# One 1 MB load for four column groups, instead of two 512 KB loads for two each, in the modulation rows of a two-block network

## The chip, the cores and the metric

The kernel runs on one core of a Trainium2 chip. The metric is device time in microseconds: the time from the first to the last instruction of one launch, as the median of several runs.

## The reference

The network has two blocks. The first one is two layers of attention and a mixture of experts over 512 tokens of width 1024. The second one is two layers of mixers and feed-forward, and every layer of it is modulated by rows that depend on two small vectors, c and c_ctx. The change is in the computation of these rows alone:

```python
xc = ctx
for layer in range(DEPTH):
    mod = jax.nn.silu(c) @ w_ada[layer] + b_ada[layer]
    sh1, sc1, g1, sh2, sc2, g2 = jnp.split(mod[:, None, :], 6, axis=-1)
    modc = jax.nn.silu(c_ctx) @ w_ada[layer] + b_ada[layer]
    sh1c, sc1c, g1c, sh2c, sc2c, g2c = jnp.split(modc, 6, axis=-1)
    u = modulate(rmsnorm(x, norm_mix_g[layer]), sh1, sc1) @ w_in[layer]
    ...
```

Each layer has 6144 columns of float32 weights over 1024 rows, 25 MB, so 50 MB are read for four rows of results. Around it, and at the same time, runs the first layer of the first block: a sliding window attention of 512 tokens, with 16 query heads and 4 key heads, and a projection of its output.

## The kernel before

The program is traced by Python functions, and a list scheduler then sets the order of instructions on every engine (the context is opened with `schedule_with_timeline_sim=True`). Engines run their own queue in order. SyncE (SP) issues the loads and stores, also in order, so an issue that waits for a buffer holds up all issues behind it.

`whole` calls `swa` (the attention of the first layer), and then `ada` on a second stream of work, `beside`, which lies on the other side of SBUF and has two banks of PSUM, a and b. The scheduler mixes both: between the products of the attention stand those of `ada`. The attention has three parts: the projections of q, k and v (products called mm<-wh,xTh and so on, L232 to L234), the heads themselves (sc<-kT,qT L377, softmax, transposes tp<-cst,pm L424, and po<-pT,v L429), and `out_proj` (mm<-wh,oTh), which ends in a layer norm and the router. Its weights w_o come as eight loads of 512 KB through three buffers. Then the experts follow: `stream` and `weights_of` load their weights; 24 granules called we lie in bytes on the second stream's side and can be loaded before the experts begin. The routing ends in a gather of token rows on GpSimd (L746), which the experts' first product (L795) needs.

`ada` keeps silu(c) and silu(c_ctx) as columns of a tile sT, padded to 32 columns. For each of the two layers and of three parts of 2048 columns it takes eight steps k over the rows. In a step, two loads of 1024 columns (512 KB, four buffers named g) are followed by two products each. A product has sT as its weights, 32 columns wide, and 512 columns of g as the moving operand; its result lies on 32 partitions of the bank (q = 0, 32, 64 or 96), so that the four 512-column pieces of a part fill the bank's 128 partitions. Each float32 product is two instructions of TensorE in the trace. The products are traced at high priority. After the eighth step the bank is added to the biases (row, L1001), and the rows go to DRAM (mod<-row), from where `columns` reads them back (mrow<-mod).

Of the kernel before, what the change touches and what calls it, by code (L numbers as in the profile page):

```python
# [11 lines left out]
F32 = mybir.dt.float32  # L12
# [11 lines left out]
def shape_constants():  # L24
    """Packed [128, n] float32 constants that depend on shapes alone: name -> array."""
# [67 lines left out]
CONST_AT = {}  # name -> group, first column, columns  # L93
# [11 lines left out]
def bcast_rows(ap, n, parts=128):  # L105
    """[n] of DRAM read by every partition."""
    return bass.AP(tensor=ap.tensor, offset=ap.offset, ap=[[0, parts], [1, n]])


def finished(steps):  # L110
    """what a generator returns at its end"""
    while True:
        try:
            next(steps)
        except StopIteration as end:
            return end.value


def together(main, rest):
    """the steps of main, and between them as many of rest as main asks for"""  # L120
# [9 lines left out]
class Net:  # L130
# [10 lines left out]
    def beside(self):  # L141
        """a second stream of work on the other side of SBUF, with two banks of PSUM"""
# [5 lines left out]
    def after(self, engine="PE"):  # L148
        """work traced under what the result returns does not come before what an engine has so far"""
# [8 lines left out]
    def new_x(self):  # L158
        """the four token tiles, in 16 KB that the attentions' outputs use in between"""
        x = self.hp.tile([128, 4, 1024], F32, name="x", tag="x")  # L160
        return [x[:, t] for t in range(4)]
# [16 lines left out]
    def dma(self, out, src):  # L178
        """a load; those of the stream beside go first, as few as they are"""
# [4 lines left out]
    def granule(self, shape):  # L184
        """4 KB of a partition for streamed weights"""
        return self.wp.tile(shape, F32, name="w", tag="w")

    def load_w(self, src, size=1024):
        """src: DRAM AP [128, kc, n] -> per k the two parts [128, n]"""
# [18 lines left out]
    def psum(self, es, **banks):  # L208
        """PSUM for a phase: 2 banks per kind of use, or as told"""
# [5 lines left out]
    def stage(self, whp=0, side=None):  # L215
        """SBUF pools of one stage, on bytes that other stages use at other times"""
# [8 lines left out]
    def split(self, hi, lo, src):  # L225
        """src (float32, SBUF or PSUM) -> hi + lo, both float32r"""
# [9 lines left out]
    def transpose_in(self, tiles, T):  # L236
        """token tiles [128, 1024] -> x^T parts [128, 8, T]"""
# [12 lines left out]
    def dense_tok(self, aT, w, tiles, kc, n, tag="mm"):  # L250
        """aT: parts [128, kc, T]; w: parts; yields (tile index, psum [128, n])"""
# [8 lines left out]
    def rstd(self, var, eps, n=1, scale=1.0):  # L260
        """(scale var + eps) ** -0.5, [128, n]: a first guess from the exponent, then a cubic iteration and Newton's (u: 2/3 of the root)"""
# [28 lines left out]
    def layer_norm(self, x, sums, gb, ta, tb, eps=1e-5):  # L290
        """x [128, 1024] in place; sums: the sum of each row in one or two parts; ta, tb: scratch"""
# [11 lines left out]
    def rope_half(self, out, src, cos, sin, nh, rot, off):  # L303
        """rotate [.., off:off+rot] of src [128, nh, d] into out; cos, sin [128, rot]"""
# [11 lines left out]
    def swa(self, xt):  # L316
        """xt in place; the logits of the experts' router"""
# [10 lines left out]
    def _swa(self, xt, oT):  # L328
# [36 lines left out]
        def attend(s, qT, t):  # L365
            """heads 8s .. 8s+7 of token tile t"""
# [26 lines left out]
    def sink_softmax(self, pm, mx, nh, nk, scale, sink=None):  # L393
        """pm [128, nh, >=nk] masked raw scores, mx raw maxima -> probabilities in place"""
# [21 lines left out]
    def pv(self, pm, nh, nk, v_of, out):  # L416
        """o^T of nh heads (pairs of 64 rows) = sum over key tiles -> out"""
# [15 lines left out]
    def out_proj(self, oT, w_o, i, xs):  # L433
        """the token tiles xs <- layer_norm(alpha x + o @ w); the logits of the experts' router"""
# [24 lines left out]
    def router(self, x, wr, lg):  # L459
        """logits of a token tile"""  # L460
# [12 lines left out]
    def token_parts(self, aT):  # L473
        """a^T [128, 8, T] -> per token tile its two parts [128, 8, 128]"""
# [6 lines left out]
    def reload(self, t):  # L481
        """a token tile from DRAM"""
# [5 lines left out]
    def mla(self, xt):  # L488
        """the new token tiles -> xd; the logits of the experts' router"""
# [1376 lines left out]
```

## Time and profile before

| | |
|---|---|
| time, median of 3 runs | 3500.92 us (3488.79 to 3513.75) |
| span of the profiled execution | 3507.8 us |
| PE busy in the span | 3240.1 us, 92% |
| DVE, ACT, POOL busy | 1666.1, 1164.3, 242.5 us |
| DMA moved | 716.17 MB, mean 204 GB/s |
| mean granted clock of TensorE | 0.963 of full speed |

No time outside the span was recorded for the profiled execution; its span is 0.2% over the median. The change lies in the first 300 us: `ada` begins its products at 23.4 us and ends them at 245 us, the output projection ends at 299 us, and the first expert's product starts at 336 us. Up to there PE is busy almost without a break. In the rows, "idle before" stands in square brackets behind a row with the engine or transfer that ended it.

### The profile page before, as it was taken

Reading aid. Unit: us, or ns where it says so; the run is one execution under the profiler, and the core shown is the slowest. Engines: PE = TensorE matmul, PEld = TensorE weight load, DVE = VectorE, ACT = ScalarE, POOL = GpSimd, SP = SyncE. Lnnn points to the kernel's source line nnn. Section 1 sums busy time; section 2 is a strip of 40 time slices with the busy share of each in tenths; the row PEclk is TensorE's granted clock in tenths of the full one; section 3 lists DMA queues with packets and bytes.
Section 4 is the critical chain, followed back from the end, with each engine's and each line's share of the span. In section 5 each row is a group of like instructions: output and inputs, shape, how many; then the busy total and the mean of one; then the engine's idle time right before and its main releaser. Section 6 shows DMA issues by size and latency. Waiting matters only on the chain. (4 is left out here: it accounts for less than half of the span.)

```text
span 3507.8 us, 48762 instructions
## 1 busy us (share of the span) xinstructions
PE 3240.1 (92%) x18404; PEld 2183.5 (62%) x18404; DVE 1666.1 (47%) x4004; ACT 1164.3 (33%) x2216; POOL 242.5 (7%) x318
## 2 busy tenths in 40 slices
PE   9987999999979979999989859999999899989998
PEld 5445344544476645666625447767888787678887
DVE  2354224223266544544524156556555556655555
ACT  3231212223155414323223144345242443443322
POOL 0000101000000010010010000130000000400000
PEclk9998999999999979999999979989999999899999
DMA  7778998999851489998899932223233232233331
GB/s 255 253 234 342 372 371 310 340 337 340 322 181 32 158 301 304 315 333 273 278 347 351 357 107 79 74 72 108 85 96 92 82 89 71 66 100 94 95 95 55
DMA packets 428088, 716.17 MB, mean 204 GB/s; under 512 B 42984, under 2 KB 283672, under 8 KB 427848
## 3 DMA queue, kind: packets, MB, share of 16 engines
q1 hardware_dynamic: 412872, 691.98, 57.3%
q0 software_dynamic: 14976, 21.02, 2.6%
q8 instruction: 147, 2.41, 0.3%
q14 instruction: 93, 0.76, 0.1%
HBM read 691.76 MB, written 37.87 MB: 208 GB/s over the span
## 5 line engine op out<-in xcount | busy, mean ns | idle before, releaser
L228 DVE TENSOR_TENSOR wl<-w,wh 128x1024 fp32r<-128x1024 f32 (+3 forms) x360 | 425.3, 1188 | 298.1 <-ACT wh L227 275.5
L227 ACT CAST wh<-w 128x1024 fp32r<-128x1024 f32 (+3 forms) x360 | 362.6, 1016 | 585.1 <-PE po L234 148.9
L795 PE MATMUL sc<-wx,xg 128*64 128x512 f32 x1492 | 437.3, 603 | 7.6 <-DMA wx<-in_moe_w_up 7.0
L232 PE MATMUL mm<-xTh,wh 128*128 128x512 f32 (+1 forms) x672 | 262.3, 390 | 1.6 <-ACT xTh L227 1.1
L234 PE MATMUL mm<-xTh,wl 128*128 128x512 f32 (+1 forms) x672 | 261.4, 389 | 1.0 <-DVE wl L228 1.0
L233 PE MATMUL mm<-xTl,wh 128*128 128x512 f32 (+1 forms) x672 | 260.6, 388 | 0.0
L795 PEld LDWEIGHTS sc<-wx,xg 128*64 128x64 f32 x1492 | 121.5, 137 | 193.9 <-issue 158.5
L232 PE MATMUL po<-wh,gTh 128*128 128x256 f32 (+1 forms) x608 | 183.4, 302 | 6.1 <-ACT gTh L227 3.9
L233 PE MATMUL po<-wl,gTh 128*128 128x256 f32 (+1 forms) x608 | 182.1, 300 | 0.0
L234 PE MATMUL po<-wh,gTl 128*128 128x256 f32 (+1 forms) x608 | 182.0, 301 | 0.0
L732 POOL DMA_INDIRECT acc<-y,to x64 | 103.7, 1620 | 1048.4 <-ACT y L809 1013.3
L807 PE MATMUL mm<-wx,hT 128*64 128x512 f32 x580 | 156.8, 657 | 11.5 <-DVE hT L803 7.9
L798 DVE TENSOR_TENSOR hid<-hid,sc 64x512 f32<-64x512 f32 x64 | 44.3, 692 | 236.3 <-ACT hid L797 235.7
L232 PEld LDWEIGHTS mm<-xTh,wh 128*128 128x128 f32 x672 | 127.7, 190 | 32.6 <-issue 2.3
L234 PE MATMUL sc<-xTh,wl 128*128 128x512 f32 (+1 forms) x384 | 145.6, 379 | 0.0
L232 PE MATMUL sc<-xTh,wh 128*128 128x512 f32 (+1 forms) x384 | 145.5, 379 | 0.0
L234 PEld LDWEIGHTS mm<-xTh,wl 128*128 128x128 f32 x672 | 127.7, 190 | 28.5 <-DVE wl L228 1.5
L233 PE MATMUL sc<-xTl,wh 128*128 128x512 f32 (+1 forms) x384 | 145.1, 378 | 0.0
L233 PEld LDWEIGHTS mm<-xTl,wh 128*128 128x128 f32 x672 | 127.6, 190 | 27.1 <-issue 0.7
L232 PE MATMUL a<-xTh,wh 128*128 128x256 f32 (+2 forms) x472 | 139.3, 295 | 2.1 <-ACT wh L227 0.9
L234 PE MATMUL a<-xTh,wl 128*128 128x256 f32 (+2 forms) x472 | 135.5, 287 | 0.8 <-DVE wl L228 0.8
L797 ACT ACTIVATE hid<-sc 64x512 f32<-64x512 f32 x64 | 37.7, 590 | 294.5 <-PE sc L795 294.3
(510 smaller groups left out, 6770.2 us busy)
## 6 DMA issues: line engine op xcount, KB each, us to landing
wx<-in_moe_w_up SPq DMA_DIRECT2D x192, 512.0 KB
wx<-in_moe_w_gate SPq DMA_DIRECT2D x181, 512.0 KB
wx<-in_moe_w_down SPq DMA_DIRECT2D x145, 512.0 KB
w<-in_ffn_w_up SPq DMA_DIRECT2D x264, 256.0 KB
g<-in_w_ada SPq DMA_DIRECT2D x96, 512.0 KB
w<-in_moe_w_down SPq DMA_DIRECT2D x76, 512.0 KB
w<-in_w_in SPq DMA_DIRECT2D x70, 512.0 KB
w<-in_ffn_w_down SPq DMA_DIRECT2D x64, 512.0 KB
```

The costliest lines, as they stand in the source:

```text
L227: self.nc.scalar.copy(hi, src)
L228: self.nc.vector.tensor_tensor(lo, src, hi.bitcast(F32), op=ALU.subtract)
L232: mm(ps, ah, bh, start=start, stop=False)
L233: mm(ps, ah, bl, start=False, stop=False)
L234: mm(ps, al, bh, start=False, stop=stop)
L732: nc.gpsimd.indirect_dma_start(out=acc, out_offset=bass.IndirectOffsetOnAxis(ap=ix, axis=0), in_=y, in_offset=None, bounds_check=1023, oob ...
L795: nc.tensor.matmul(ps[r], xg[:, k], w, start=k == 0, stop=k == 7)
L797: nc.scalar.activation(hid[64:], ps[:64], AF.Silu)
L798: V.tensor_tensor(hid[64:], hid[64:], ps[64:], op=ALU.mult)
L807: nc.tensor.matmul(py[64 * h:64 * h + 64], hT[:, k], w[:, 512 * h:512 * h + 512], start=k == 0, stop=k == 3)
```

## The change

A step now has one load of 2048 columns (1 MB, as a tile of 4 by 512 columns) and four products, one for each 32-partition group, traced one after another. There are two buffers of 8 KB a partition each in place of four of 4 KB, so the bytes are the same. Comments and docstrings were taken out as well, which moves line numbers by three below it (the products' line is L993 after, L995 before; the load's L990 and L991).

```diff
-            wp = self.pool(es, "adw", 4)
+            wp = self.pool(es, "adw", 2)
...
                 for b in range(3):
                     ps = self.bank("mm")
                     for k in range(8):
-                        for h in range(2):
-                            c = 2048 * b + 1024 * h
-                            g = wp.tile([128, 1024], F32, name="g")
-                            nc.sync.dma_start(g, w[:, k, c:c + 1024])
-                            with self.tc.high_priority():
-                                for a in range(2):
-                                    q = 64 * h + 32 * a
-                                    nc.tensor.matmul(ps[q:q + 32], sT[:, k], g[:, 512 * a:512 * a + 512], start=k == 0,
-                                                     stop=k == 7)
+                        g = wp.tile([128, 4, 512], F32, name="g")
+                        nc.sync.dma_start(g, w[:, k, 2048 * b:2048 * b + 2048].rearrange("p (a n) -> p a n", a=4))
+                        with self.tc.high_priority():
+                            for a in range(4):
+                                nc.tensor.matmul(ps[32 * a:32 * a + 32], sT[:, k], g[:, a], start=k == 0, stop=k == 7)
```

The scheduler writes another order. On PE, the products of `ada` (a<-g,sT) stand in 87 places before and in 47 after; 18 of the 48 steps now stand among the projections and up to the first scores, 27 in the heads' part and 3 in the output projection, where before all of them stood ahead of the output projection. From the experts on, the products of PE are the same, with some of the second stream's moved by some places among those of the first layer's experts.

In the heads' part of the attention, PE stood in this order before:

```order
L995 MATMUL a<-g,sT 32x512 x2
L377 MATMUL sc<-kT,qT 128x256
L424 MATMUL tp<-cst_58,pm 128x128 x4
L995 MATMUL a<-g,sT 32x512 x4
L429 MATMUL po<-pT,v 64x128 x4
L377 MATMUL sc<-kT,qT 128x256 x2
L995 MATMUL a<-g,sT 32x512 x2
```

The same engine after, at the same place:

```order
L993 MATMUL a<-g,sT 32x512 x4
L377 MATMUL sc<-kT,qT 128x256 x2
L429 MATMUL po<-pT,v 64x128 x8
L993 MATMUL a<-g,sT 32x512 x4
L377 MATMUL sc<-kT,qT 128x256 x2
L424 MATMUL tp<-cst_58,pm 128x128 x8
L993 MATMUL a<-g,sT 32x512 x4
```

Blocks of four products now stand about twice as far apart as the blocks of two did.

SP's queue at the end of `ada`, before (w_o are the output projection's weights, prow, mrow and cols belong to `columns`, we are the experts' weights):

```order
L181 DMA prow<-in_gla_norm_g 1x64 x2
L439 DMA wr<-in_moe_w_group 128x8x4
L440 DMA wr<-in_moe_w_expert 128x8x32
L181 DMA w<-in_a_w_o 128x2x512 x3
L181 DMA cols<-col 128x320
L832 DMA we<-in_moe_w_gate 128x1024
```

And after, first at the last loads of `ada` and then some 20 rows further on:

```order
L990 DMA g<-in_w_ada 128x2048
L181 DMA w<-in_a_w_o 128x2x512
L990 DMA g<-in_w_ada 128x2048
L181 DMA w<-in_a_w_o 128x2x512 x4
L181 DMA mrow<-mod 16x128 x2
```

```order
L181 DMA mrow<-mod 16x128
L181 DMA mod<-row 2x512 x2
L287 DMA w<-in_ln_g 128x1024
L287 DMA w<-in_ln_b 128x1024
L832 DMA we<-in_moe_w_gate 128x1024
L832 DMA we<-in_moe_w_up 128x1024
```

The last five loads of w_o moved ahead of the small transfers of `columns`, and the first experts' weights moved behind the two loads of the layer norm, which before stood among them.

At the ends of the eight-step sums, SP's queue before:

```order
L991 DMA g<-in_w_ada 128x1024 x16
L181 DMA mod<-row 2x512 x4
L991 DMA g<-in_w_ada 128x1024 x3
L181 DMA row<-in_b_ada 32x512 x4
L991 DMA g<-in_w_ada 128x1024 x13
```

And after:

```order
L990 DMA g<-in_w_ada 128x2048 x8
L181 DMA mod<-row 2x512 x4
L990 DMA g<-in_w_ada 128x2048
L181 DMA row<-in_b_ada 32x512 x4
L990 DMA g<-in_w_ada 128x2048 x7
```

One load of two buffers now stands between the stores of a finished part and the bias loads of the next one, where three of four buffers did.

## Rows read from the trace of the kernel before

**Rows 1.** Busy time in four stretches: length, engines with (instructions), clock, DMA share, GB/s.
```profile
23.30:118.90 95.60, 95.60 (x409) 51.66 (x408) 21.19 (x55) 20.43 (x33) 0.00 (x0) 1.00 0.73 245
118.90:245.30 126.40, 119.80 (x739) 48.68 (x740) 67.57 (x315) 47.63 (x176) 0.00 (x0) 1.00 0.81 259
245.30:299.10 53.80, 49.23 (x218) 38.78 (x218) 26.64 (x61) 12.77 (x16) 0.00 (x0) 0.97 0.86 321
299.10:336.30 37.20, 14.65 (x146) 12.98 (x144) 22.58 (x87) 5.78 (x10) 2.28 (x2) 0.68 0.79 300
```

**Rows 2.** The same view for the instructions of tile g alone (PE, PEld).
```profile
23.30:118.90 95.60, 32.42 (x128) 4.57 (x128) 1.00 0.73 245
118.90:245.30 126.40, 61.14 (x256) 8.56 (x256) 1.00 0.81 259
```

**Rows 3.** PE in order of time: start, us, engine, line, operation, count.
```profile
44.26 0.39 PE L233 MATMUL mm<-wl,xTh 128*128 128x512 f32 x1
44.58 1.05 PE L995 MATMUL a<-g,sT 128*32 128x512 f32 x4
45.56 0.50 PE L234 MATMUL mm<-wh,xTl 128*128 128x512 f32 x1
45.90 0.39 PE L232 MATMUL mm<-wh,xTh 128*128 128x512 f32 x1
46.13 0.39 PE L233 MATMUL mm<-wl,xTh 128*128 128x512 f32 x1
...
118.91 1.06 PE L995 MATMUL a<-g,sT 128*32 128x512 f32 x8
```

**Rows 4.** Who PE waited for, 118.9 to 245.3: us in total, times, longest.
```profile
PE a L995 <- DMA g<-in_w_ada: 6.0, 5, 2.3
```

**Rows 5.** The same for PE's weight loads, its two longest waits for softmax.
```profile
PEld sc L377 <- DVE pm L414: 5.5, 9, 0.8
PEld sc L377 <- DVE mx L379: 5.1, 8, 0.8
```

**Rows 6.** SP and PE in order of time, around a load that PE waited for.
```profile
197.26 1.06 PE L995 MATMUL a<-g,sT 128*32 128x512 f32 x8
198.36 4.11 SPq L991 DMA_DIRECT2D g<-in_w_ada  x4
199.48 1.05 PE L995 MATMUL a<-g,sT 128*32 128x512 f32 x4
...
201.05 1.05 PE L995 MATMUL a<-g,sT 128*32 128x512 f32 x4
...
204.92 1.05 PE L995 MATMUL a<-g,sT 128*32 128x512 f32 x4 [1.60 <-DMA g<-in_w_ada]
```

**Rows 7.** SP around the output projection, in order of time.
```profile
253.91 1.54 SPq L181 DMA_DIRECT2D w<-in_a_w_o  x3
...
258.95 0.42 SPq L832 DMA_DIRECT2D we<-in_moe_w_gate  x1
...
277.06 0.33 SPq L287 DMA_DIRECT2D w<-in_ln_b  x1
```

**Rows 8.** ACT there: the split of w_o's fourth granule.
```profile
258.56 1.04 ACT L227 CAST wh<-w 128x1024 fp32r<-128x1024 f32 x1 [9.04 <-DMA w<-in_a_w_o]
```

**Rows 9.** PE there.
```profile
259.66 0.74 PE L232 MATMUL mm<-wh,oTh 128*128 128x512 f32 x2 [2.10 <-ACT wh L227]
260.92 0.65 PE L233 MATMUL mm<-wl,oTh 128*128 128x512 f32 x1 [0.52 <-DVE wl L228]
```

**Rows 10.** Busy time in two stretches there, columns as in rows 1.
```profile
262.00:264.00 2.00, 2.00 (x6) 1.51 (x6) 1.11 (x3) 0.00 (x0) 0.00 (x0) 0.50 0.98 336
260.00:300.00 40.00, 39.48 (x171) 31.57 (x169) 20.64 (x49) 8.51 (x11) 0.00 (x0) 0.96 1.02 397
```

**Rows 11.** GpSimd's first gather, and the first expert's product, in order of time.
```profile
322.93 1.26 POOL L746 DMA_INDIRECT x<-xd,slots  x1 [322.50 <-DMA wx<-in_moe_w_up]
...
336.29 1.09 PE L795 MATMUL sc<-we,xg 128*64 128x512 f32 x2
```

## Prediction

> **What bounds the kernel now.** I read the busy time by stretches first, since shares of the whole span say nothing of a stage that ends after 300 us. From the first product of `ada` to the first scores PE is busy for 95.60 of 95.60 us, and in the heads' part for 119.80 of 126.40 us, both at full clock [rows 1]. In the heads' part DVE works 67.57 us and ACT 47.63 us, so neither is near its limit, and the DMA engines move 245 and 259 GB/s, where with deep queues they move 397 [rows 1, 10]. PE idles for 6.6 us of the heads' part, and 6.0 of these are waits of `ada`'s products for their weights [rows 4]. So PE bounds these 222 us, and whatever leaves its queue shortens them, until loads or the softmax come late. What `ada` holds of PE is 32.42 + 61.14 = 93.56 us [rows 2]: more than a third of the two stretches, for 48 steps.
>
> **Four groups at once.** A block of two products takes 1.05 us (four instructions). Where two such blocks happen to be neighbours, eight instructions take 1.06 us [rows 3]: all four column groups run beside each other, and the second pair costs 0.01 us. The change makes every step such a block. 48 x 1.06 = 50.9 us in place of 93.56: **-42.7 us**, all of it on the engine that sets the end.
>
> The Trainium skill (TensorE: Matmul & The Clock Gate, Part 3: Packing small matmuls) gives the span of a pack as one matmul plus some 4 ns for each further tile, but lists only 2.38 times for three column groups, 79% of three. By that share a block of four would take about 1.06 / 0.79 = 1.34 us, an estimate, and 13 us of the gain would go. The trace agrees with the span and not with the share: 1.06 against 1.05 us.
>
> **Fewer changes between the two kinds of products.** From 44.26 to 45.90 one ordinary product, one block and one ordinary product begin in turn: 1.64 us; two ordinary steps of 0.23 us (45.90 to 46.13) off, the block costs 1.18, that is 0.13 more than its own 1.05 [rows 3]. 87 places become 47: 40 x 0.13 = **-5.2 us**. Together -47.9.
>
> **Loads.** Bytes in flight stay at 2 MB, but two buffers hold them. A buffer's loop is load, block, next load. No row shows a 1 MB load. The lower bound is from a load that finds the DMA engines idle: the first of three 512 KB loads of w_o is issued at 253.91 and its split begins at 258.56, 4.65 us [rows 7, 8]. The other 512 KB at 397 GB/s add 1.3: 5.95, with the block 7.0, so two buffers give a step every 3.5 us. The upper bound is a load that PE waited for: the block at 197.26 held two buffers and freed them for the loads from 198.36 on; after two more blocks, at 204.92, PE waits for the first of these: 6.56 us [rows 6]. With 1.3 and 1.06 that is 8.9, a step every 4.46 us.
>
> Against this stands PE's own work per step. Projections: (95.60 - 32.42) / 18 steps = 3.51, with the block's 1.19 it is 4.70 us, above both bounds, so no wait there beyond unlucky spacing. Heads: (119.80 - 61.14) / 27 = 2.17, with 1.19 it is 3.36 us, below both [rows 1, 2]. The waits of the heads' part are thus between 27 x 0.14 = 4 us and 27 x 1.10 = 30 us. I take 13, nearer to the lower bound, because at most one other load can stand ahead of a load now, where three could. In this lies also that at the five ends of eight-step sums only one load stands in SP's queue between the stores of mod and the bias loads, which wait for these stores. 6.0 us of waits are there today: **+7 us** net, from -6 (all hidden) to +24.
>
> The Trainium skill (DMA: Bandwidth & Descriptors, Rules for kernel authors) asks for 1 MiB or more a DMA for full bandwidth. By it the larger loads would be faster in themselves, and the waits would go as in the first rival below, 3451 us. The trace shows 397 GB/s with loads of mostly 512 KB [rows 10], so I give the size no credit.
>
> **Softmax.** With PE's part of the heads at 27 x 3.36 = 91 us, plus waits some 104, DVE's 67.57 us become 65% of it, in chains from scores to transposes. Today these waits end under running products: the two longest groups of weight loads that wait for DVE hold 10.6 us, with next to no idle PE [rows 5]. Blocks of `ada` that took two places between scores and transposes take one now, so some cover is gone: **+4 us**, from 0 to 11.
>
> **Output projection.** Today w_o's fourth granule is issued late, behind the small transfers of `columns`; PE waits 2.10 and 0.52 us for its split [rows 9], and then runs at half clock (0.50, the 1.2 GHz level, from 262 to 264), after these idle times, which costs at least 1.0 us more [rows 10]. After the change it is issued ahead of them. But the last two blocks of `ada` stand within this projection, and the very last load is issued only behind that granule, which waits for the split of the first one: **-2 us**, from -3.6 to +4.
>
> **The experts' weights.** In SP's queue their first loads now stand behind ln_b, today at 277.06, instead of at 258.95 [rows 7]: 18 us later in the projection. What covers it: the DMA engines idle for 21% of the 37.2 us from 299.1 to 336.3, 7.8 us [rows 1], and the first product on these weights comes at 336.29 [rows 11]. What isn't covered goes behind the routing's gather (322.93 to the product, 13.4 us, in part queueing behind such loads): **+4 us**, from 0 to 18 - 7.8 = 10.
>
> **Later.** Some products of the second stream change places among the first layer's experts, where PE and DMA are both nearly full: 0, from -10 to +10. Everything after that keeps its order and moves with the stage.
>
> **Sum.** -47.9 + 7 + 4 - 2 + 4 = -35 us. The span of the profiled execution, 3507.8, is 0.2% over the median of 3500.9, which moves the sum by less than 0.1 us: **3466 us**, 0.990 of the time before.
>
> **Rivals.**
> 1. The loads stay hidden. Then the waits of today go too: -47.9 - 6 - 2 + 4 + 2 (softmax) = -50, 3451 us. For it: the steps are spread evenly in the order. Against it: 3.36 us of work per step is below even the lower bound of the loop. 17%.
> 2. The two-buffer loop takes over, **slower**. If both loads in flight share the DMA engines, a load takes 6.56 + 1.3 for its own second half + 1.3 for the other's; with the block 10.2 us, 5.1 us a step. The 45 steps ahead of the output projection then take 230 us where 222 pass now: +8, with the experts' weights +12, 3513 us. It decides from 222 / 45 = 4.93 us a step on. For it: SP's loads wait for PE already, so nothing runs ahead. Against it: the 6.56 us hold the queueing behind three loads. 7%.
> 3. The groups don't run four at once, when weights of one load stand in one tile: 48 x 2 x 1.05 is more than today's 93.56 and takes back the switching; with hidden loads it comes to about -6, 3495 us. The eight-fold row speaks against it: 4%.
> 4. The gain is made in the heads and given back: the experts' weights and the gather cost their full 10, and the reordered experts 10: -19, 3482 us. Both engines are nearly full there, so nothing catches up. 20%.
>
> **How the numbers follow.** The forecast has 52%. A measurement of this kernel tells a change from none at about 1%, 35 us, which is where the forecast lies. So half of its chance and nearly all of the first rival's is faster by over 1%: 0.43. Slower by over 1% needs a step of well over 5.1 us: 0.05, part of the second rival and what I don't see. The rest, 0.52, is within 1%. The low end of the range has waits, softmax and projection at their best, -47.9 - 6 - 3.6, 3444 us. The high end has loads, softmax and experts' weights at their worst, -47.9 + 24 + 11 - 2 + 10 = -5, with a little for the reordered experts 3498 us.
>
> **What would show it.** In the trace after: blocks of eight instructions of 1.06 us, and some 51 us for tile g's products (else rival 3); the heads' part ending 30 to 45 us before 245.3; PE's waits for g in the heads' part at 4 to 30 us, where under 4 is rival 1 and over 40 rival 2; the fourth granule of w_o no longer waited for; the time from there to the first expert's product, 91.0 us today (245.3 to 336.3), a few us longer; equal stages after the first experts. The prediction is wrong if the gain of the first stretch is there and the first expert's product doesn't come earlier, or if the experts' part changes its length by more than 10 us.

## The result, and the profile after

The changed kernel takes 3458.8 us, the median of 4 runs (3454.3 to 3466.0), where the kernel before took 3500.8 (4 runs on the same chip): 0.9856 of the time, with a 95% interval from 0.983 to 0.9882. That is 42 us less; the forecast was 35 less. The profiled execution has a span of 3464.2 us, 43.6 less than the 3507.8 of before.

**Where the 43.6 us came from** can be read off four points that both kernels pass: the output projection's first product (PE, tile oTh), the first expert's product, the first copy of the next attention's keys (DVE, `kk<-kr`), and the end. In us from the span's start, for all kernels of this study:

| kernel | projection | first expert | keys copied | end | to first expert | experts' part | rest |
|---|---|---|---|---|---|---|---|
| before | 247.7 | 336.3 | 1031.7 | 3507.8 | 88.6 | 695.4 | 2476.1 |
| after | 212.2 | 307.0 | 992.9 | 3464.2 | 94.8 | 685.9 | 2471.3 |
| after_again | 209.7 | 306.0 | 993.8 | 3458.0 | 96.3 | 687.8 | 2464.2 |
| consts_act | 215.7 | 313.6 | 999.0 | 3458.5 | 97.9 | 685.4 | 2459.5 |
| two_pairs | 242.6 | 330.0 | 1025.5 | 3505.2 | 87.4 | 695.5 | 2479.7 |
| small_loads | 217.2 | 303.3 | 1006.7 | 3473.5 | 86.1 | 703.4 | 2466.8 |
| three_bufs | 209.9 | 298.7 | 993.5 | 3463.9 | 88.8 | 694.8 | 2470.4 |
| ln_own | 214.2 | 312.3 | 1007.6 | 3479.0 | 98.1 | 695.3 | 2471.4 |
| w4 | 214.5 | 307.5 | 1005.4 | 3478.6 | 93.0 | 697.9 | 2473.2 |
| consts_w4 | 212.5 | 305.4 | 1000.7 | 3480.0 | 92.9 | 695.3 | 2479.3 |
| one_group | 204.8 | 309.0 | 1009.4 | 3481.0 | 104.2 | 700.4 | 2471.6 |
| one_buffer | 203.9 | 440.9 | 1139.2 | 3602.2 | 237.0 | 698.3 | 2463.0 |
| four_buffers | 169.6 | 395.5 | 1085.8 | 3562.2 | 225.9 | 690.3 | 2476.4 |

The changed kernel is 35.5 us ahead when the projection begins, loses 6.2 up to the first expert, gains 9.5 in the experts' part and 4.8 in the rest.

**The first 35.5 us.** Busy time by stretch, as in [rows 1], now up to the first scores, up to the projection's first product, to the end of its products, and to the first expert's product:

```profile
23.60:99.00 75.40, 75.27 (x387) 49.38 (x386) 20.44 (x54) 19.96 (x32) 0.00 (x0) 1.00 0.77 280
99.00:212.20 113.20, 96.23 (x749) 47.82 (x748) 67.88 (x316) 49.77 (x180) 0.00 (x0) 0.98 0.82 289
212.20:264.90 52.70, 52.41 (x250) 39.84 (x251) 29.68 (x67) 12.03 (x15) 0.00 (x0) 1.00 0.78 287
264.90:307.00 42.10, 14.19 (x122) 12.74 (x120) 20.42 (x80) 5.18 (x9) 2.27 (x2) 0.57 0.92 367
```

The same view for tile g alone, as in [rows 2]:

```profile
23.60:99.00 75.40, 14.92 (x112) 2.20 (x112) 1.00 0.77 280
99.00:212.20 113.20, 33.32 (x248) 5.01 (x248) 0.98 0.82 289
```

In the first two stretches tile g's products hold 48.24 us for 45 steps; the last three steps now stand behind the projection's first product. That is 45.3 less than the 93.56 of before [rows 2]. PE's idle time there is 0.13 + 16.97 = 17.1 us, 9.1 more than the 8.0 of the kernel before up to its projection; PE's other products hold some 0.6 us more. Together this is the 35.5 us, but for rounding and a start that is 0.3 later.

The two stretches are not those of [rows 1]. The first scores of the kernel before come at 129.61 us and not at 118.9:

```profile
129.61 0.48 PE L377 MATMUL sc<-kT,qT 64*128 64x128 f32 x2
```

and those of the changed kernel at 99.04:

```profile
99.04 0.48 PE L377 MATMUL sc<-kT,qT 64*128 64x128 f32 x2
```

By the 112 and 248 instructions of tile g, 14 steps stand ahead of the first scores and 31 between them and the projection, not 18 and 27, as the section on the change and the prediction have it. PE's order of time shows the blocks, as in [rows 3]:

```profile
48.28 0.40 PE L234 MATMUL mm<-wh,xTl 128*128 128x512 f32 x1
48.61 1.06 PE L993 MATMUL a<-g,sT 128*32 128x512 f32 x8
49.60 0.50 PE L232 MATMUL mm<-wh,xTh 128*128 128x512 f32 x1
49.94 0.39 PE L233 MATMUL mm<-wl,xTh 128*128 128x512 f32 x1
```

Every step is a block of eight instructions that takes 1.06 us: four products for the time of one. From 48.28 to 49.94 are 1.66 us; without two ordinary steps of 0.23 they are 1.20, so a place where the kinds change costs 0.14, as it did before [rows 3].

Who PE waited for between 23.6 and 212.2, as in [rows 4] (in all, times, longest):

```profile
PE a L993 <- DMA g<-in_w_ada: 13.5, 13, 2.1
PE po L429 <- DVE pT L426: 1.4, 2, 0.9
PE sc L377 <- DVE mx L379: 1.3, 3, 0.6
```

The waits for g are 13.5 us. The softmax is late for 2.7 us of idle PE in these rows, where it was 0.4 before; PE's weight loads wait 5.4 us for `mx` and 3.0 for `pm`, where [rows 5] has 5.1 and 5.5.

**The projection.** ScalarE's split of w_o's fourth granule, which answers to [rows 8], and PE's first product there, which answers to [rows 9]:

```profile
212.24 0.74 PE L232 MATMUL mm<-wh,oTh 128*128 128x512 f32 x2 [0.42 <-ACT wh L227]
219.88 1.05 ACT L227 CAST wh<-w 128x1024 fp32r<-128x1024 f32 x1 [5.80 <-DMA w<-in_a_w_o]
```

ScalarE still waits for that granule, 5.80 us, but no product of the projection waits for it any more: PE idles for 0.3 of its 52.7 us.

**Up to the first expert.** DVE of the changed kernel in order of time; `cst` here are the routing constants of the first MoE layer:

```profile
277.85 0.17 DVE L849 TENSOR_SCALAR gs<-gs 128x4 f32<-128x4 f32 x1
282.77 0.23 DVE L626 CAST 128b<-cst 128x128 bf16<-128x128 f32 x1 [4.75 <-DMA cst<-in_consts]
```

SP issues the load of these constants at this time in the kernel before:

```profile
299.33 0.33 SPq L181 DMA_DIRECT2D cst<-in_consts  x1
```

and at this in the changed one:

```profile
272.88 0.33 SPq L181 DMA_DIRECT2D cst<-in_consts  x1
```

That was 51.6 us after the projection's first product, and is now 60.6 us after it; DVE waits 4.75 us for it, in the middle of the routing. The gather and the first expert's product, as in [rows 11]:

```profile
294.50 1.25 POOL L746 DMA_INDIRECT x<-xd,slots  x1 [294.07 <-DMA wx<-in_moe_w_gate]
...
306.99 3.52 PE L795 MATMUL sc<-we,xg 128*64 128x512 f32 x12
```

From the gather to the product are 12.5 us now and 13.4 before: the gather did not become slower. What became slower is the routing ahead of it. From the start of the row `gs<-gs` (L849) above to the slots of the gather (L700) DVE takes 15.5 us now (277.85 to 293.38), and took 9.5 before (312.33 to 321.81).

### The profile page after: what moved, and what is told of

It reads as the page before. It is cut to its first block, busy times and chain, and to the rows that moved or that the text cites. A ratio compares the mean times of both kernels' runs of the same rounds, so it can differ in the third digit from the quotient of the medians.

```text
span 3464.2 us, 48671 instructions
## 1 busy us (share of the span) xinstructions
PE 3182.9 (92%) x18404; PEld 2178.4 (63%) x18404; DVE 1666.0 (48%) x4004; ACT 1165.7 (34%) x2217; POOL 241.4 (7%) x318
```

## The experiments

All ratios are to runs of the kernel before on the same chip and in the same group of runs, where its median lay between 3500 and 3516 us.

**1. The packing alone undone (two_pairs).**

```
- for a in range(4):
-     nc.tensor.matmul(ps[32 * a:32 * a + 32], sT[:, k], g[:, a], start=k == 0, stop=k == 7)
+ for a in range(4):
+     q = a % 2 if k else a
+     nc.tensor.matmul(ps[32 * q:32 * q + 32], sT[:, k], g[:, a], start=k == 0, stop=a > 1 and k in (0, 7))
```

Expected: 

> Undoes only the side-by-side part: loads of 1 MB and two buffers stay, but from the second step of a sum on the third and fourth products go into the first two column groups, so two pairs follow each other (the sums of parts three and four are thus added to those of one and two: that part of the computation is changed). Theory 'the four groups are the gain': a step costs two blocks of 1.05 us, tile g's products take 42 x 2.10 + 6 x 1.06 = 95 us instead of 51.4, PE's work per step in the heads' part rises by 1.05 to about 4.4 us, which hides the loads, so the 13.5 us of waits for g fall under 5; the output projection's first product comes at 212 + 44 - 9 = 247 us, and the time is about 3490. Rival 'the 1 MB loads are the gain': the output projection starts before 220 us and the time stays under 3467.

Measured: 3498.2 us, 0.9953 of the time before (0.9931 to 0.9975), 17 us less than the kernel before in this group; the projection starts some 4 us earlier than the theory said. PE in order of time:

```profile
124.18 1.91 PE L994 MATMUL a<-g,sT 128*32 128x512 f32 x8
...
127.19 1.05 PE L994 MATMUL a<-g,sT 128*32 128x512 f32 x4
```

The group of all products of tile g (busy time, mean ns, idle time before them):

```profile
L994 PE MATMUL a<-g,sT 128*32 128x512 f32 x384 | 87.7, 605 | 5.7 <-DMA g<-in_w_ada 5.4
```

Two pairs on the same column groups take 1.91 us where four groups side by side take 1.06. PE's waits for g fall from 13.5 to 5.4, since each step now gives the next load 0.85 us more. The projection starts at 242.6: of the 35.5 us, 30.4 go with the packing. The other 5.1 stay, although the loads are those of the changed kernel: 87.7 against 93.6 us of products, because two pairs back to back cost less than two pairs apart.

**2. The loads alone undone (small_loads).**

```
- g = wp.tile([128, 4, 512], F32, name="g")             # adw with 2 buffers
- nc.sync.dma_start(g, w[:, k, 2048 * b:2048 * b + 2048]...)
+ gs = []                                               # adw with 4 buffers
+ for h in range(2):
+     c = 2048 * b + 1024 * h
+     g = wp.tile([128, 2, 512], F32, name="g")
+     nc.sync.dma_start(g, w[:, k, c:c + 1024]...)
+     gs.append(g)
- for a in range(4):
+ for a in (2, 3, 0, 1):                                # the second load's products first
...
```

Expected: 

> Undoes only the load: each step has two loads of 512 KB into four buffers of half the size, and the four products follow each other once both are in. The scheduler puts the experts' first loads ahead of ln_b again, as in the kernel before. Theory 'the size of a load matters little, bytes in flight and the number of steps in flight do': waits for g within 4 us of 13.5, the output projection's first product at 208 to 216 us, and 3452 to 3462 in all, the lower end if the experts' weights were worth their 4 to 6 us. Rival 'a load of 1 MB moves faster in itself': waits for g over 20 us, the projection's start at 219 us or later, over 3465.

Measured: 3473.9 us, 0.990 (0.986 to 0.9939). The waits are those of the theory; the start of the projection, 217.2, lies between the two expectations, and the time is above the theory's range, though the kernel before too took 15 us more in this group than in that of the result. The group of its products and their waits:

```profile
L997 PE MATMUL a<-g,sT 128*32 128x512 f32 x384 | 52.9, 623 | 15.3 <-DMA g<-in_w_ada 13.8 <-DVE sx_r L412 1.4
```

The waits for g are those of the changed kernel, 13.8 against 13.5, so the larger load is not what shortens or lengthens them. The projection starts 5.0 us later than in the changed kernel: 47 steps stand ahead of it here and not 45, so that tile g's products hold 3.5 us more there (51.75 against 48.24), and PE's other products 2.2. Up to the first expert it takes 86.1 us, 8.7 less than the changed kernel: in this order the constants aren't waited for. Then 17.5 us go in the experts' part (703.4 against 685.9).

**3. A third buffer (three_bufs).**

```
- wp = self.pool(es, "adw", 2)
+ wp = self.pool(es, "adw", 3)
- with self.stage(whp=5):        # the stage of projections and heads
+ with self.stage(whp=4):
```

Expected: 

> Three buffers of 1 MB instead of two; room for the third comes from one pair of split weights less in the first layer's projections and heads (four instead of five). Theory 'the loop of load and block over two buffers makes the waits': with three, the loop of 7.0 to 8.9 us gives a step every 2.3 to 3.0 us, under the 3.36 us of PE's work, so waits for g fall from 13.5 to under 4 us and the output projection's first product comes at about 202 us. The order of w_o and the experts' weights changes too and may take up to 5 back: 3449 to 3454. Rival 'the DMA engines themselves are late' (their share is 0.84 in the heads' part): waits for g stay over 9 us, the projection's start at 208 or later, 3456 or more.

Measured: 0.9864 (0.9833 to 0.9896), the same as the changed kernel; the projection starts at 209.9 us and not at the 202 of the theory. The group of products of tile g:

```profile
L993 PE MATMUL a<-g,sT 128*32 128x512 f32 x384 | 50.9, 604 | 0.8 <-DMA g<-in_w_ada 0.4 <-DVE row L998 0.4
```

The heads' part in two stretches, up to `ada`'s last product and on to the projection, columns as in [rows 1]:

```profile
87.50:190.50 103.00, 100.29 (x724) 51.05 (x723) 58.52 (x279) 41.46 (x151) 0.00 (x0) 1.00 0.91 331
190.50:209.90 19.40, 14.17 (x112) 9.86 (x104) 12.87 (x55) 10.05 (x35) 0.00 (x0) 0.82 0.36 124
```

The waits for g are gone (0.4 us), as the loop of two buffers says, and the DMA engines carry 331 GB/s without being late: the rival falls. But the projection starts only 2.3 us earlier than in the first execution of the changed kernel, and no earlier than in the second (209.7, experiment 5). The last product of `ada` now begins at 190.5, and for the 19.4 us from there PE has little but the softmax's own chain: it is busy for 14.17 us, at a granted clock of 0.82. Up to the projection the sum is: 13.1 us of waits for g less; 2.7 more of tile g's products, since all 48 steps stand ahead of the projection here; 3.9 more of other products, in part at half clock; and 4.2 more of other idle time, 2.4 of it waits for the softmax. So 13.1 us of waits were worth 2.3, or 5.0 without the three steps. That the waits had stood under the softmax's chain is argued from this sum, not shown.

The run also has one pair of split weights less. Against w4 (experiment 9), which has this and two buffers, the third buffer is a gain: the projection starts 4.6 us earlier, and the ratio is 0.9864 against 0.9937, with intervals that don't touch. So three buffers with four pairs take the same time as two buffers with five, and four pairs with two buffers take longer; no run has three buffers and five pairs.

**4. Buffers of their own for ln_g and ln_b (ln_own).**

```
- gb = [self.granule([128, 1024]) for _ in range(2)]
+ gb = [self.lp.tile([128, 1024], F32, name=f"lng{a}", bufs=1) for a in "gb"]   # first layer
...
```

Expected: 

> ln_g and ln_b of the first layer get buffers of their own, so their loads no longer wait for the projection's weight buffers, and the experts' first loads stand ahead of the small transfers. Theory 'the experts' weights behind ln_b cost what the time from the projection's first product to the first expert's product grew by (88.6 before, 94.8 after)': that time comes back to 88 to 91 us and the whole is 3453 to 3456. Rival 'the later loads are covered, and something else makes it longer': it stays within 1.5 us of 94.8, 3458 or more.

Measured: 0.9934 (0.9908 to 0.996). The experts' first load is issued at 215.4 us, 1.2 us after the projection's first product (26.5 after it in the changed kernel), and the time from there to the first expert's product grows to 98.1 us instead of falling. The theory of the expectation, which is that of the prediction's term on the experts' weights, isn't borne out: their early issue doesn't help. It is no clean test of them, though, since other things moved in this order. DVE's wait for the routing constants falls to 1.9 us, but from the projection's last product to `gs` it takes 18.2 us (13.4 in the changed kernel), and from the gather to the product 15.1 (12.5).

**5. The changed kernel again (after_again),** with no edit.

Expected: 

> The changed kernel itself, a second profiled execution, to tell what in its gain belongs to the order of the instructions and what to one execution. Theory 'the experts' part is shorter because of its new order': from the first expert's product at 307 us to the end of that stage it takes 654 us again (663.7 before), within 2 us. Rival 'it is scatter of one execution': the length moves by over 4 us. The 6 us that the first profile gained near its end, where the kernel before ran 10 us at a granted clock of 0.50 and the changed one at 1.00, I expect to be scatter: it may be absent here, and the span then nearer 3470.

Measured: 0.9873 (0.9832 to 0.9915). The experts' part takes 687.8 us where the first execution took 685.9 and the kernel before 695.4. So the gain of 7.6 to 9.5 us there goes with the order, as far as one execution of the kernel before can show it. PE's waits for g up to the projection are 10.9 us here, where they were 13.5, and the projection starts 2.5 us earlier: in one and the same order these waits cost about their full length. The rest of the program takes 2464.2 us against 2471.3. One place of it, columns as in [rows 1], in the first execution:

```profile
2240.00:2248.00 8.00, 8.00 (x31) 5.33 (x31) 3.19 (x13) 2.90 (x10) 2.39 (x6) 0.50 0.00 0
```

and in the second:

```profile
2240.00:2248.00 8.00, 8.00 (x59) 5.54 (x58) 6.55 (x29) 4.29 (x16) 4.48 (x6) 1.00 0.47 95
```

PE is busy throughout in both, but once at the 1.2 GHz level with 31 instructions and once at 2.4 GHz with 59. The same shows some 760 us later between the kernels. Before:

```profile
3000.00:3010.00 10.00, 10.00 (x38) 6.37 (x37) 4.46 (x20) 3.12 (x12) 2.69 (x7) 0.50 0.00 1
```

The changed kernel, in its first execution, at the same place of the program:

```profile
2962.40:2972.40 10.00, 9.82 (x68) 6.84 (x68) 8.36 (x40) 6.17 (x23) 5.83 (x12) 1.00 0.18 32
```

And the changed kernel in its second execution, at this place:

```profile
2952.40:2962.40 10.00, 10.00 (x37) 6.73 (x38) 5.09 (x24) 3.28 (x11) 2.83 (x7) 0.50 0.00 1
```

So the kernel before ran both places at 0.50 (the first one from 2276 to 2288), and each execution of the changed kernel one of them, not the same one. The 4.8 us that the rest of the program seemed to gain are of the size of one such place and less than what two executions of one program differ by, 7.1: nothing shows that the change has part in them.

**6. The routing constants from ScalarE's queue (consts_act).**

```
- self.load_consts(self.php, 3)
+ self.load_consts(self.php, 3, None if i else self.nc.scalar)   # the queue that issues the load
...
```

Expected: 

> The changed kernel, with the first layer's routing constants loaded from ScalarE's queue instead of SyncE's, where they stand behind 19 loads of the experts' weights. Theory 'what the projection-to-expert time grew by is the wait of DVE for these constants' (4.75 us, from 278.0 to 282.8): the wait goes, and the first expert's product comes 4 to 6 us earlier, at 301 to 303 us; the whole 3453 to 3455. Rival 'the DMA engines are full there (0.92), so the constants land late from any queue': the wait stays over 3 us and the first expert's product stays at 305 to 308 us.

Measured: 0.9879 (0.9834 to 0.9923), no gain, and the first expert's product at 313.6, later than both expectations. ScalarE and its queue in order of time:

```profile
277.59 0.38 ACTq L170 DMA_DIRECT2D cst<-in_consts  x1
278.07 1.15 ACT L301 ACTIVATE ln_b<-x,ln_n 128x1024 f32<-128x1024 f32 x1 [10.28 <-DMA we<-in_moe_w_down]
```

DVE no longer waits for the constants, but the issue itself stood on ScalarE, by the trace until a load of the experts' weights was done, and a layer norm stood behind it for 10.28 us. The wait moved from DVE to ScalarE and doubled: 97.9 us to the first expert. The queue was the wrong cure. PE's order in the experts' part is that of the changed kernel here, and that part takes 685.4 us, a third time within 2.4 us.

**7. One buffer (one_buffer)**: `adw` with 1 buffer.

Expected: 

> One buffer of 1 MB instead of two: it shows the length of the loop by itself, since in the heads' part each block then waits for a load that was only issued after the block ahead of it. Theory 'the loop is 7.0 to 8.9 us, as worked out from the loads of w_o and from the block that waited': the blocks of the heads' part begin every 7.0 to 8.9 us, and each waits for most of the difference to PE's work. Rival 'a 1 MB load takes longer when it shares the engines, loop 10.2 us': every 9.5 us or more. Since the order then holds only 24 blocks ahead of the output projection, the rest comes among the experts; the whole is 3470 to 3520.

Measured: 3604 us, one run (before: 3508.6), far outside the 3470 to 3520 expected. PE's blocks in order of time:

```profile
126.42 1.07 PE L993 MATMUL a<-g,sT 128*32 128x512 f32 x8
132.37 1.07 PE L993 MATMUL a<-g,sT 128*32 128x512 f32 x8 [0.24 <-DMA g<-in_w_ada]
138.47 1.49 PE L993 MATMUL a<-g,sT 128*32 128x512 f32 x8 [0.50 <-DMA g<-in_w_ada]
```

The loop is 5.95 and 6.10 us: below both of my bounds. Without the block of 1.06 a load of 1 MB takes 4.9 to 5.0 us from its issue to its use, hardly more than the 4.65 us of one with 512 KB [rows 7, 8]. Half of the steps move behind the projection in this order: it starts at 203.9 us, but the first expert comes 237.0 us after it, 148 more than before, and with this the whole is 95 us longer.

**8. Four buffers (four_buffers)**: `adw` with 4 buffers.

Expected: 

> Four buffers of 1 MB. They need 16 KB more a partition, for which there is no room beside the first layer's projections and heads, so all 48 steps move behind the heads, into the output projection and the experts' part. Theory 'the steps cost PE the same wherever they stand, and beside the experts they also cost the DMA engines, which are full there': the output projection starts at 155 to 175 us, the heads' part now being set by the softmax, but 48 MB more at some 400 GB/s, 126 us, are loaded beside the experts' weights, and the whole is slower than the changed kernel, 3480 to 3530. Rival 'the experts' part has room for them': under 3460.

Measured: 3564 us, one run, longer than both expectations. With no room for them beside the heads, all steps move behind the projection's first product, which comes at 169.6, where the heads end without them; the first expert comes only at 395.5. The largest of PE's waits between 300 and 420 us:

```profile
PE a L993 <- DMA g<-in_w_ada: 23.6, 22, 2.8
```

The blocks there wait for loads that share the DMA engines with the experts' weights. The place beside the heads is worth more than the buffers.

**9 and 10. Four pairs of split weights (w4), and with the constants loaded at the start (consts_w4).**

```
- with self.stage(whp=5):              # both: the stage of projections and heads
+ with self.stage(whp=4):
+ self.load_consts(self.pool(early, "c3", 1), 3)     # consts_w4: ahead of the first layer
- self.load_consts(self.php, 3)                      # consts_w4: now for the second layer alone
...
```

Expected of w4: 

> The changed kernel with four pairs of split weights instead of five in the first layer's projections and heads, and nothing else: the control for the next run and for the run with three buffers. The routing constants still stand in SyncE's queue behind the experts' weights. Theory 'the fifth pair hides nothing here': waits for g 10 to 15 us, the output projection's first product at 210 to 214 us, DVE's wait for the constants 3 to 6 us, the first expert's product at 303 to 308 us. Rival 'the fifth pair is what let the run with three buffers gain only 2 us': waits for split weights in the projections, and the output projection's start at 215 us or later.

Expected of consts_w4: 

> As w4, and the routing constants of the first layer are loaded at the kernel's start into a buffer of their own (the room is that of the fifth pair); the rest of SyncE's order is that of w4. Theory 'the wait of DVE for these constants is what the time from the projection to the first expert grew by': the wait is gone, and this time is 4 to 6 us shorter than in w4, near the 88.6 us of the kernel before. Rival 'the gather is late too, behind the experts' weights': the time from the router's last product to the first expert's product shrinks by under 2 us.

Measured: 0.9937 (0.9914 to 0.9961) and 0.9927 (0.9899 to 0.9955). Up to the projection the fifth pair hides little: waits for g are 11.0 us, and the projection starts at 214.5. Yet w4 is slower than the changed kernel: 3483.8 us (3474.1 to 3490.2) against 3463.0 (3459.8 to 3473.2) on the same chip. In the profiles 10 to 12 us of this are in the experts' part, in another order; why is open. Of DVE's waits in w4 the constants' is

```profile
DVE 128b L626 <- DMA cst<-in_consts: 5.3, 1, 5.3
```

and in consts_w4 there is none: from `gs` to the slots it takes 9.5 us there, as in the kernel before and in three_bufs, where the constants aren't waited for either. Yet the time to the first expert is 93.0 and 92.9 us. The products of the router's last tiles, PE in order of time, in w4:

```profile
269.70 1.98 PE L470 MATMUL sc<-wr,xTr 128*128 128x36 f32 x16 [0.25 <-ACT xTr L467]
```

and in consts_w4:

```profile
272.25 1.76 PE L470 MATMUL sc<-wr,xTr 128*128 128x36 f32 x8
273.82 1.09 PE L466 MATMUL tp<-cst,x 128*128 128x128 f32 x4
274.73 3.63 PE L470 MATMUL sc<-wr,xTr 128*128 128x36 f32 x16
```

Eight products of the router take 0.98 us in the one (16 in 1.98) and 1.76 in the other, with a granted clock of 1.00 (262 to 275) and of 0.50 (266 to 279). So the router's last result came late in consts_w4, and what the constants' wait gave back went there. So it is shown that DVE waits for the constants, and not that the kernel gets 5 us faster without that wait.

**11. One product in place of four (one_group).**

```
- for a in range(4):
+ for a in range(1 if k else 4):
...
```

Expected: 

> The changed kernel with three of each step's four products left out, but for the first step of a sum (so three quarters of these sums lack seven of their eight terms); the loads are unchanged. Theory 'a block costs what one product costs, the others ride along': the blocks of one product still take 1.05 to 1.06 us, tile g's products 50 to 52 us in all, and the output projection's first product comes within 3 us of the changed kernel's 209.7 and 212.2. Rival 'each further column group costs its own share' (a third of the block or so): blocks of 0.6 to 0.8 us, 29 to 38 us in all, and the projection's start 8 us or more earlier, if the loads don't take that up in waits.

Measured: 3482.8 us, one run (before on the same chip: 3515.9). PE in order of time:

```profile
46.57 1.04 PE L993 MATMUL a<-g,sT 128*32 128x512 f32 x2
```

The group of products of tile g:

```profile
L993 PE MATMUL a<-g,sT 128*32 128x512 f32 x132 | 51.2, 611 | 7.1 <-DMA g<-in_w_ada 6.1 <-DVE pm L414 1.0
```

132 instructions take 51.2 us here, 384 take 51.4 in the changed kernel: three more column groups cost nothing. The projection starts at 204.8, 4.9 to 7.4 us earlier and so outside the 3 us that I gave; the waits for g are 7.4 us shorter here, in an order of its own. DVE waits 9.5 us for the constants in this one, the longest of all.

No version here beats the changed kernel by more than its interval; three_bufs equals it.

## Why the prediction came out right, step by step

**Four groups at once** (-42.7): 93.6 became 51.4 us, -42.2. The eight-fold row of before [rows 3] was the whole evidence, and it held for all steps. Experiments 1 and 11 show the mechanism from both sides: two pairs on the same groups cost 1.91 us, and leaving three of four products out saves nothing. Rival 3 is out. The Trainium skill (TensorE: Matmul & The Clock Gate, Part 3: Packing small matmuls) gives a pack's span as one matmul and some 4 ns for each further tile; 1.06 against 1.04 us, with four products and with one, agrees.

**Fewer changes between kinds** (-5.2): a place costs 0.14 us, as worked out, but the sum isn't there. PE's busy time without tile g is 216.3 - 93.6 = 122.7 us up to the projection before (95.60 + 119.80 [rows 1], and 0.9 up to 247.7) and 171.5 - 48.2 = 123.3 after. 0.9 us of the latter are transposes at half clock (below). Among the projections the term is there: 30 places became 14, and the other products up to the stretch's end hold 60.35 us in place of 63.18 [rows 1, 2], of which about 1.1 are six products that now stand further on. In the heads' part, with 57 places become 30, they didn't get shorter. So at most 2 us came, and this term was oversized by 3 or more: a price read between projections was taken for the heads too.

**Loads** (+7 net, waits of 13): 13.5 - 6.0 = +7.5 (+4.9 in the second execution), the size that I took, but not by the working that I gave; that it fits is luck. The loop is 6.0 us and not 7.0 to 8.9: I had added 1.3 us for the second 512 KB to the lower bound, and experiment 7 shows that a 1 MB load takes hardly longer. Two buffers thus give a step every 3.0 us. PE's work per step was wrong as well, since the split into 18 and 27 steps was: from the first scores to the projection PE is busy for 96.23 us with 31 steps, 3.10 a step and not 3.36. So the loop is no longer than the work, and the argument that I held against rival 1 falls; but there is next to nothing to spare either, so any unevenness becomes a wait. I see two. The blocks are not evenly spread: PE in order of time,

```profile
119.12 1.06 PE L993 MATMUL a<-g,sT 128*32 128x512 f32 x8
121.96 1.06 PE L993 MATMUL a<-g,sT 128*32 128x512 f32 x8
125.08 1.06 PE L993 MATMUL a<-g,sT 128*32 128x512 f32 x8 [0.83 <-DMA g<-in_w_ada]
```

the third of these could have begun 5.13 us after the first and begins 5.96 after it, one loop. And at the ends of the sums SP's queue is held up. SP in order of time:

```profile
140.06 2.69 SPq L181 DMA_DIRECT2D row<-in_b_ada  x4
142.80 1.29 SPq L990 DMA_DIRECT2D g<-in_w_ada  x2
```

PE at the same time:

```profile
139.34 1.07 PE L993 MATMUL a<-g,sT 128*32 128x512 f32 x8 [0.60 <-DMA g<-in_w_ada]
142.62 1.06 PE L993 MATMUL a<-g,sT 128*32 128x512 f32 x8
147.67 1.06 PE L993 MATMUL a<-g,sT 128*32 128x512 f32 x8 [1.70 <-DMA g<-in_w_ada]
```

The block at 139.34 is done at 140.4, but the load into its buffer is issued at 142.80, behind the bias loads; 4.87 us later PE has it. Rival 2 is out with the loop: 3.0 us a step is far from its 5.1.

The Trainium skill (DMA: Bandwidth & Descriptors, Rules for kernel authors) wants 1 MiB or more a load for the highest bandwidth. Experiment 7 agrees, 4.9 us for 1 MB against 4.65 for 512 KB, but experiment 2 shows the same waits with loads of half the size: with 2 MB in flight either way, the kernel hardly feels it.

**Softmax** (+4): 2.7 us of idle PE in the rows above, 2.3 more than before. Experiment 3 shows the limit that the term spoke of: with the loads hidden, part of what they gave goes into waits for the softmax. Rival 1's sum was too good: three_bufs has its premise, no waits, and by its terms (-47.9 - 6 + 2) the projection would start at 196 us; it starts at 209.9.

**Output projection** (-2): from its first product to its last it takes 52.2 us (212.2 to 264.4), 51.0 before (247.7 to 298.7), with three blocks of `ada` in it (I had counted two), 3.2 us, that stood ahead of it before. Without these it is 2.0 shorter, as worked out; PE's waits for the granule's split are gone [rows 9].

**The experts' weights** (+4): the 5 us are there, from the projection's last product to the first expert's (264.4 to 307.0, 42.6, against 298.7 to 336.3, 37.6), but the carrier is another one. It isn't the gather, and issuing the weights early doesn't help (experiment 4). It is one small load, the routing constants, that stands behind them in the same queue, and for which DVE waits 4.75 us (6.2 in the second execution): the routing from `gs` to the slots grew by 6.0 us (7.5), and the other parts of the way did not grow. In [rows 7] I had looked at which loads move back, and not at which load nobody would prefetch.

**Later** (0, from -10 to +10): -9.5 and -7.6 in the two executions, in the bound, but not at its middle. Three executions with the changed order give 685.4 to 687.8 us, other orders 690.3 to 703.4. What in the order does it stays open. Rival 4 had the sign the other way round: 10 us lost there.

**The sum.** Up to the first expert the forecast said about -35 and it was -29.3, which is what the terms measured here add up to without that of the kinds: -42.2 + 7.5 + 2.3 - 2.0 + 5.0 = -29.4. The term that came out wrong in size is this one, -5.2, of which the sum shows next to nothing; the experts' order gave 9.5 back and the rest of the program 4.8, which nothing puts down to the change. That the forecast missed the time by only 7 us rests partly on these two.

## What to carry to other kernels

Count a block of narrow products by its longest column group, not by its products: four groups of 32 columns cost what one costs, and one place in the old trace where two pairs happen to meet is enough to price the change. Before giving waits a price, look at what stands under them: a third buffer took 13.1 us of waits for weights away, and the next stage began 2.3 us earlier, because three more steps and waits for the softmax took their place. When loads are moved back in a queue, look for the small load behind them that the next engine needs, and try a place ahead for it, rather than another queue that has to wait for the same loads; no run here got faster by that alone.

## What the runs showed that I had not expected

After a stretch with idle time the clock can stay low for a time that differs from one execution to the next, with the same program: from 2240 to 2248 us PE was busy throughout at 0.50 in one execution and at 1.00 in the other, after 24 us in which it had been busy for 20.0 and 20.3. Such places help to make the time from the keys' copy to the end scatter between 2459.5 and 2479.7 us over all these kernels, whose code is the same there; that is half of the gain that was to be measured.

It also fell after a shorter pause. PE waited 2.08 us for `ada`'s weights until 205.70 and was busy for 0.30 of the 2 us from 204 on; in the next 2 us the granted clock was 0.53. The changed kernel, columns as in [rows 1]:

```profile
204.00:206.00 2.00, 0.30 (x4) 0.16 (x8) 1.32 (x5) 0.03 (x1) 0.00 (x0) 1.00 0.98 377
206.00:208.00 2.00, 2.00 (x12) 0.81 (x5) 0.00 (x0) 0.00 (x0) 0.00 (x0) 0.53 0.79 332
```

The block at 205.70 took 1.57 us in place of 1.06, and eight transposes after it 1.97 in place of 1.09. The second execution has the same: a wait of 2.23 us until 203.04, and 0.52 from 204 to 206. A wait for weights costs more than its length when the clock goes with it.
